# A hybrid flow-matching backbone: the high parts of the mixers' weights come by a second, casting load

## The chip, the cores and the metric

One NeuronCore of a Trainium2 chip runs the whole kernel. The metric is the device time of one execution in microseconds (us). The kernel before takes 2733.23 us (median of 3 runs, 2732.98 to 2734.27).

## What is computed

The reference is a backbone of four layers on 256 latent tokens and 256 context tokens, 1024 features wide. Cut to what matters here:

```python
for i in range(4):
    mod_l, mod_c = silu(c) @ ada_w[i] + ada_b[i], silu(c_ctx) @ ada_w[i] + ada_b[i]   # six vectors each
    h  = modulate(rmsnorm(x, norm_mix[i]), shift, scale)         # context and latents
    o  = (gated_deltanet, rglru, hgrn2)[i % 3](h @ w_in, ...) @ w_out
    x  = x + gate * o
    x  = x + gate2 * (silu(h2 @ w1) * (h2 @ w3)) @ w2            # h2 = modulated rmsnorm of x
return rmsnorm(x_latents, norm_final)
```

Layers 0 and 3 mix the tokens by a gated DeltaNet, layer 1 by the RG-LRU, layer 2 by HGRN2. The last layer needs the latents alone at its end. All inputs and weights are float32.

## The kernel before

Features lie along the 128 partitions, the 512 tokens along the free dimension. Every dense product is carried by three products of split operands: an operand is its high part, rounded to float32r, plus a low part, the exact rest. `dense` (L162 to L173) takes one slab of weights, 128 rows by 8 blocks of 128 columns (512 KB), and for each of 8 blocks multiplies high by high (L170), low weights by high tokens (L171) and high weights by low tokens (L172): 24 matmuls for a slab.

The slabs come in a fixed order, which `plan` writes down. For each slab `load` (L93) sends one DMA on SyncE's queue into one of 4 `raw` tiles. `fetch` (L110) splits it: a copy to the tile `whi` gives the high part, on ScalarE (L123) or, within the RG-LRU's blocks, on VectorE (L121, `hi_dve`); a subtraction on VectorE, raw less `whi`, gives the tile `wlo` (L124). There are 3 tiles `whi` and 3 `wlo`. Splits run 2 slabs ahead of the slab in use and loads 4 slabs ahead, so the `whi` of slab n+2 takes the tile of slab n-1 and has to wait for the last matmul of that one. The projections of the DeltaNet take their slabs with no splitting ahead and call `fetch` after the convolution that follows (L634, L642).

The mixers use 41 slabs of weights in layer 0, 28 in layer 1, 48 in layer 2 and 41 in layer 3 (their input, gate and output weights). The feed-forward parts use 68 slabs a layer (`w13`, `w2`). Beside these, the modulation weights `ada` come through the same 4 `raw` tiles in layer 0's mixer (48 loads in all before and in it, the first 16 into tiles of their own), where TensorE multiplies them by silu(c) (L286); the later layers' ada weights come beside a feed-forward part, into tiles of their own.

The order of the instructions of each engine's queue is set when the program is built, by a scheduler that goes by its own estimate of each instruction's time; within the RG-LRU's blocks ScalarE keeps the order of the program text. On the chip each queue runs in that order, and an instruction that waits holds up what is queued behind it. GpSimd issues no DMA in this kernel. It does elementwise work: products with a sigmoid (L535), masks (L245), products in HGRN2 (L1237, L1238, L1255) and in the RG-LRU (L1046, L1081, L1113, L1122), and half of the norms' products (L385).

Of the kernel before, what the change touches and what calls it, by code (L numbers as in the profile page):

```python
"""Hybrid flow-matching backbone on one NeuronCore.

Everything runs feature-major: a stream of 512 tokens (256 context, then 256 latent) lies along
the free dimension, features along the partitions in blocks of 128. Dense float32 products are
carried by three single-pass float32r products of exactly split operands.
"""
# [14 lines left out]
P = 128  # L21
KT = 8
T = 512
# [31 lines left out]
class Net:  # L55
# [9 lines left out]
    # ---------------------------------------------------------------- weights  # L65
    AHEAD, AHEAD_RAW = 2, 4

    def plan(self):
        """Every slab of weights, in the order in which the layers take them."""
# [33 lines left out]
    def take(self, *key, ahead=None):  # L103
        """The next slab [128 k, kt x 128 n] as high and low parts; later ones are set going."""
        assert self.wplan[self.wpos][0] == key[0] and self.wplan[self.wpos][1] == key[1:], (key, self.wplan[self.wpos])
        self.wpos += 1
        self.fetch(self.AHEAD if ahead is None else ahead)
        return self.wready.pop(0)

    def fetch(self, ahead=AHEAD):  # L110
        """Loads and splits of the slabs up to `ahead` past the last one taken."""
        nc = self.nc
        n = len(self.wplan)
        while self.wsplit_at < min(n, self.wpos + ahead):
            while self.wload_at < min(n, self.wsplit_at + 1):
                self.wload()
            t, w = self.wraw.pop(0)
            hi = self.p_w.tile([P, 1024], F32R, tag="whi", name=self.nm("whi"))
            lo = self.p_w.tile([P, 1024], F32R, tag="wlo", name=self.nm("wlo"))
            if self.hi_dve:  # L120
                nc.vector.tensor_copy(hi[:, :w], t[:, :w])  # L121
# [8 lines left out]
    def wload(self):  # L130
# [8 lines left out]
        self.wraw.append((self.load(src, w), w))  # L139
        self.wload_at += 1  # L140

    # ---------------------------------------------------------------- building blocks
# [17 lines left out]
    def dense(self, w, hs, t0=0, t1=T, ps=None):  # L160
        """ps[n, t] = sum_k w[k, n] h[k, t] over the blocks of hs = [(hi, lo)]."""
# [13 lines left out]
    def dense2(self, k1, k2, hs, ps1, ps2):  # L175
        """Two dense products, both for the context first: its half of hs is there earlier."""
# [6 lines left out]
    def gather(self, po):  # L183
        """A product that adds to a part of the bank po. The first one makes all of the bank ready
        to be written, so the others stay behind it."""
# [16 lines left out]
    def sigmoid(self, out, in_):  # L202
        """1 / (1 + exp(-x)) from the table set that also has the logarithm."""
# [5 lines left out]
    # ---------------------------------------------------------------- constants  # L209
    def consts(self, pool):  # L210
# [11 lines left out]
        # column s adds up over the partitions  # L222
# [12 lines left out]
        # allowed [p, i]: i >= p forwards, i <= p backwards  # L235
# [5 lines left out]
    def causal(self, out, in_, d, n, chunks=1, fill=0.0):  # L241
        """out[p, .., i] = in_ where i >= p (forwards) or i <= p (backwards), else fill."""
# [4 lines left out]
    # ---------------------------------------------------------------- modulation  # L247
    def ada(self, i, summed):
        """Generator: the six modulation vectors of layer i, a piece of the weights at a time.

        Either by products, or (summed) on the vector engine, which leaves the sum over the
        partitions to the products."""
# [3 lines left out]
        for g in range(3):  # L256
# [22 lines left out]
            else:  # L279
                # half of the columns of both vectors at a time: the first blocks of features go on early  # L280
# [11 lines left out]
    def ada_out(self, i, g, ps, js):  # L292
        """The vectors' blocks js from the rows 32 j of the bank ps, feature-major and with their bias."""
# [19 lines left out]
    def step_ada(self, n=1):  # L313
        """Up to n steps."""
# [7 lines left out]
    # ---------------------------------------------------------------- norms  # L322
# [6 lines left out]
    def stats_add(self, n, s):  # L329
        """Squares of the feature block n, stream s, as soon as it is final."""  # L330
# [12 lines left out]
    def rstd(self, s):  # L343
        """1 / sqrt(mean over the features + eps) of stream s, on every partition."""
# [9 lines left out]
    def behind(self, ins, first):  # L354
        """Keep ins behind an earlier instruction of its engine."""
# [1091 lines left out]
```

## Time and profile before

| | |
|---|---|
| median of 3 runs | 2733.23 us |
| span of the profiled execution | 2732.4 us, 0.8 us under that median; the page gives no other time for it |
| TensorE matmul busy | 2576.3 us, 94% of the span |
| VectorE busy | 1846.4 us, 68% |
| ScalarE busy | 1257.2 us, 46% |
| GpSimd busy | 330.1 us, 12% |
| moved by DMA | 373.66 MB, 137 GB/s over the span |

The span falls into eight stretches: a mixer and its output product, then a feed-forward part, for each layer. The mixers lie at 0 to 475 us (layer 0), 835 to 1050 (layer 1), 1411 to 1806 (layer 2) and 2170 to 2530 (layer 3); the feed-forward parts lie between them and at the end. A stretch is read from the table of busy times, which engine is nearly always busy in it, and from the chain of work that ended last, which says what each step was released by. Names carry the layer and stage: L1m is the mixer of layer 1, L3kq the keys and queries of layer 3, L0f the feed-forward part of layer 0, op an output product.

### The profile page before, as it was taken

To read this page: it belongs to the slowest core of one execution; us is meant where nothing else is said; L and a number is where in the kernel's file an instruction comes from. 1 tells how busy PE (TensorE), PEld (TensorE's weight loads), DVE (VectorE), ACT (ScalarE), POOL (GpSimd) and SP (SyncE) were. 2 spreads that over 40 slices of the span, in tenths; PEclk is the share of its full clock that TensorE was granted. 3 is DMA by queue.
4 is the path that set the end of the run, shared out by engine and by line. 5 is a ranking of instruction groups with operands and counts; after the bars stand their busy time and mean duration, and the time that the engine had idled before them with its cause. 6 is when DMAs were issued, how large, how long until landed. Compare 5 with 4: busy or idle time off the path is not lost.

```text
span 2732.4 us, 39594 instructions
## 1 busy us (share of the span) xinstructions
PE 2576.3 (94%) x15528; PEld 2137.5 (78%) x15528; DVE 1846.4 (68%) x2851; ACT 1257.2 (46%) x2075; POOL 330.1 (12%) x286
## 2 busy tenths in 40 slices
PE   7999899999999889999999999999999997788998
PEld 3676788888878668888878888788888786678998
DVE  4585866666667986766666656667666668566555
ACT  4567664322236654222245545442222465774443
POOL 1331001000002421000012122110000134110000
PEclk9999999999999989999999999999999998989999
DMA  6675432555542224555522212135555454224554
GB/s 232 209 228 167 140 122 94 162 169 176 172 140 91 77 70 124 185 169 164 175 85 78 62 62 77 56 124 183 163 177 167 130 152 123 79 70 142 163 181 129
DMA packets 129515, 373.66 MB, mean 137 GB/s; under 512 B 13712, under 2 KB 24976, under 8 KB 129328
## 3 DMA queue, kind: packets, MB, share of 16 engines
q1 hardware_dynamic: 128176, 369.03, 43.3%
q8 instruction: 122, 2.00, 0.3%
q10 hardware_dynamic: 1152, 2.10, 0.2%
q14 instruction: 65, 0.53, 0.1%
HBM read 355.28 MB, written 15.79 MB: 136 GB/s over the span
## 4 chain that ended last, share of the span: by engine, by line
PE 71%; DVE 12%; ACT 8%; DMA 4%; issue 3%; POOL 2%; SPq 0%; ACTq 0%; POOLq 0%; DVEq 0%
PE L0f_psm L172 3%; PE L0f_psm L170 3%; PE L0f_psm L171 3%; PE L2f_psm L170 3%; PE L2f_psm L172 3%; PE L1f_psm L170 3%; PE L1f_psm L172 3%; PE L2f_psm L171 3%; PE L1f_psm L171 3%; PE L3f_psm L172 1%; PE L3f_psm L171 1%; PE L3f_psm L170 1%; PE L2m_psd L172 1%; PE L0f_psd L172 1%; PE L0f_psd L170 1%
## 5 line engine op out<-in xcount | busy, mean ns | idle before, releaser
L123 ACT ACTIVATE L0f_whi<-L0f_raw 128x1024 fp32r<-128x1024 f32 (+1 forms) x58 | 61.2, 1054 | 229.0 <-issue 139.8
L123 ACT ACTIVATE L1f_whi<-L1f_raw 128x1024 fp32r<-128x1024 f32 (+1 forms) x58 | 61.2, 1054 | 228.7 <-issue 143.7
L123 ACT ACTIVATE L2f_whi<-L2f_raw 128x1024 fp32r<-128x1024 f32 (+1 forms) x58 | 61.1, 1054 | 228.7 <-issue 143.7
L269 DVE SCALAR_TENSOR_TENSOR L1f_acc<-L1f_raw,silu_c,L1f_acc 128x1024 f32<-128x1024 f32 x84 | 107.6, 1281 | 42.1 <-DMA L1f_raw<-in_ada 41.9
L269 DVE SCALAR_TENSOR_TENSOR L0f_acc<-L0f_raw,silu_c,L0f_acc 128x1024 f32<-128x1024 f32 x84 | 107.6, 1281 | 40.6 <-DMA L0f_raw<-in_ada 40.5
L269 DVE SCALAR_TENSOR_TENSOR L2f_acc<-L2f_raw,silu_c,L2f_acc 128x1024 f32<-128x1024 f32 x84 | 107.6, 1281 | 39.8 <-DMA L2f_raw<-in_ada 39.7
L124 DVE TENSOR_TENSOR L3f_wlo<-L3f_raw,L3f_whi 128x1024 fp32r<-128x1024 f32 (+1 forms) x58 | 70.5, 1216 | 50.5 <-ACT L3f_whi L123 50.5
L172 PE MATMUL L2m_psd<-hlo,L2m_whi 128*128 128x512 f32 (+1 forms) x256 | 103.7, 405 | 0.0
L123 ACT ACTIVATE L3f_whi<-L3f_raw 128x1024 fp32r<-128x1024 f32 (+1 forms) x58 | 61.0, 1052 | 91.4 <-issue 59.1
L171 PE MATMUL L2m_psd<-hhi,L2m_wlo 128*128 128x512 f32 (+1 forms) x256 | 101.2, 395 | 0.9 <-DVE L2m_wlo L124 0.9
L170 PE MATMUL L2m_psd<-hhi,L2m_whi 128*128 128x512 f32 (+1 forms) x256 | 100.0, 391 | 0.0
L171 PE MATMUL L1f_psm<-hhi,L1f_wlo 128*128 128x512 f32 (+1 forms) x248 | 95.0, 383 | 0.2 <-DVE L1f_wlo L124 0.2
L171 PE MATMUL L2f_psm<-hhi,L2f_wlo 128*128 128x512 f32 (+1 forms) x248 | 95.0, 383 | 0.2 <-DVE L2f_wlo L124 0.2
L171 PE MATMUL L0f_psm<-hhi,L0f_wlo 128*128 128x512 f32 (+1 forms) x248 | 95.0, 383 | 0.2 <-DVE L0f_wlo L124 0.2
L172 PE MATMUL L1f_psm<-hlo,L1f_whi 128*128 128x512 f32 (+1 forms) x248 | 94.9, 383 | 0.0
L170 PE MATMUL L1f_psm<-hhi,L1f_whi 128*128 128x512 f32 (+1 forms) x248 | 94.9, 383 | 0.0
L172 PE MATMUL L2f_psm<-hlo,L2f_whi 128*128 128x512 f32 (+1 forms) x248 | 94.9, 383 | 0.0
L170 PE MATMUL L0f_psm<-hhi,L0f_whi 128*128 128x512 f32 (+1 forms) x248 | 94.9, 383 | 0.0
L170 PE MATMUL L2f_psm<-hhi,L2f_whi 128*128 128x512 f32 (+1 forms) x248 | 94.9, 383 | 0.0
L172 PE MATMUL L0f_psm<-hlo,L0f_whi 128*128 128x512 f32 (+1 forms) x248 | 94.7, 383 | 0.0
L124 DVE TENSOR_TENSOR L2m_wlo<-L2m_raw,L2m_whi 128x1024 fp32r<-128x1024 f32 x38 | 50.0, 1315 | 36.3 <-ACT L2m_whi L123 36.0
L124 DVE TENSOR_TENSOR L0f_wlo<-L0f_raw,L0f_whi 128x1024 fp32r<-128x1024 f32 (+1 forms) x58 | 70.2, 1210 | 1.6 <-ACT L0f_whi L123 1.5
(1330 smaller groups left out, 8724.8 us busy)
## 6 DMA issues: line engine op xcount, KB each, us to landing
L0f_raw<-in_w SPq DMA_DIRECT2D x56, 512.0 KB, 4.4
L1f_raw<-in_w SPq DMA_DIRECT2D x56, 512.0 KB, 4.5
L2f_raw<-in_w SPq DMA_DIRECT2D x56, 512.0 KB, 4.4
L3f_raw<-in_w SPq DMA_DIRECT2D x56, 512.0 KB, 3.6
L0f_raw<-in_ada SPq DMA_DIRECT2D x48, 512.0 KB, 3.8
L1f_raw<-in_ada SPq DMA_DIRECT2D x48, 512.0 KB, 3.9
L2f_raw<-in_ada SPq DMA_DIRECT2D x48, 512.0 KB, 3.8
L2m_raw<-in_w_hin SPq DMA_DIRECT2D x36, 512.0 KB, 3.5
```

The source lines that it names most:

```text
L123: nc.scalar.activation(hi[:, :w], t[:, :w], AF.Copy)
L124: nc.vector.tensor_tensor(out=lo[:, :w], in0=t[:, :w], in1=hi[:, :w].bitcast(F32), op=ALU.subtract)
L170: mm(o, wh, hh[:, t0:t1], start=(k == 0), stop=False)
L171: mm(o, wl, hh[:, t0:t1], start=False, stop=False)
L172: self.pe_mark = mm(o, wh, hl[:, t0:t1], start=False, stop=(k == n - 1))
L269: ins = nc.vector.scalar_tensor_tensor(out=o, in0=w, scalar=c, in1=o, op0=ALU.mult, op1=ALU.add)
```

## The change

A second way to the high part is added for the slabs of the mixers: instead of the copy from `raw`, GpSimd issues a DMA that reads the same slab from HBM again and writes it as float32r, rounded on the way, into `whi`. The load into `raw` stays, and so does the subtraction for `wlo`. The feed-forward slabs keep ScalarE's copy. The flag `hi_dve` goes, and with it VectorE's copies. Comments are left out too, which changes no instruction.

```diff
+    CAST = ("w_gab", "w_gin", "w_gout", "w_lin", "w_lg", "w_lout", "w_hin", "w_hout")
...
-            t, w = self.wraw.pop(0)
+            t, w, src, cast = self.wraw.pop(0)
             hi = self.p_w.tile([P, 1024], F32R, tag="whi", name=self.nm("whi"))
             lo = self.p_w.tile([P, 1024], F32R, tag="wlo", name=self.nm("wlo"))
-            if self.hi_dve:
-                nc.vector.tensor_copy(hi[:, :w], t[:, :w])
+            if cast:
+                nc.gpsimd.dma_start(hi[:, :w], src)
             else:
                 nc.scalar.activation(hi[:, :w], t[:, :w], AF.Copy)
             nc.vector.tensor_tensor(out=lo[:, :w], in0=t[:, :w], in1=hi[:, :w].bitcast(F32), op=ALU.subtract)
...
-        self.wraw.append((self.load(src, w), w))
+        self.wraw.append((self.load(src, w), w, src, name in self.CAST))
...
-                self.hi_dve = True
                 with tc.manual_schedule(engines={mybir.EngineType.Activation}):
                     self.lru_blocks(i, t2, neg, pos, hs)
-                self.hi_dve = False
```

## Rows read from the trace of the kernel before

**Rows 1.** Busy by stretch: window, length, PE, PEld, DVE, ACT, POOL, clock, DMA share, GB/s.

```profile
0.00:475.00 475.00, 432.25 (x3089) 322.15 (x3090) 311.67 (x641) 285.01 (x510) 89.27 (x93) 0.98 0.53 171
475.00:835.00 360.00, 359.88 (x1647) 294.43 (x1647) 239.38 (x274) 102.01 (x136) 0.74 (x1) 1.00 0.52 161
835.00:1050.00 215.00, 187.96 (x871) 154.45 (x870) 188.70 (x261) 136.04 (x225) 71.20 (x47) 0.91 0.25 79
1411.00:1806.00 395.00, 379.51 (x2373) 320.47 (x2372) 259.60 (x424) 206.09 (x351) 80.12 (x67) 1.00 0.22 69
2170.00:2530.00 360.00, 301.47 (x2663) 263.41 (x2662) 250.12 (x548) 233.45 (x453) 81.42 (x76) 0.92 0.37 112
```

**Rows 2.** The same view inside layers 0, 1 and 3.

```profile
0.00:40.00 40.00, 22.60 (x85) 9.62 (x86) 19.41 (x45) 19.14 (x43) 11.10 (x21) 0.87 0.97 356
74.00:215.00 141.00, 134.46 (x657) 94.83 (x655) 104.94 (x164) 79.91 (x126) 49.56 (x45) 0.99 0.71 226
892.83:928.15 35.32, 31.29 (x126) 24.99 (x125) 34.54 (x39) 23.37 (x35) 13.88 (x9) 0.90 0.23 75
928.15:963.47 35.32, 28.32 (x115) 22.18 (x113) 34.54 (x39) 23.41 (x36) 13.84 (x9) 0.90 0.24 75
2170.00:2280.00 110.00, 100.63 (x623) 86.47 (x622) 83.72 (x154) 79.29 (x151) 44.15 (x44) 0.97 0.47 140
```

**Rows 3.** Chain that ended last, 835 to 1010 us: shares by line; then pieces (start, length, what).

```profile
by line: DVE L1m_g L1113 8.1%; DVE L1m_wlo L124 7.4%; DVE L1m_whi L121 6.9%; DVE L1m_xc L508 6.9%; issue 6.5%; DVE L1m_t L1123 5.2%; DVE L1m_t L1116 5.1%; PE L1m_psd L172 4.7%; PE L1m_psd L170 4.2%; PE L1m_psd L171 4.0%; DVE L1m_t L1119 3.9
...
893.34 1.32 DVE L1m_whi L121
...
920.78 0.69 DVE L1m_whi L121
```

**Rows 4.** Waits of PE in layer 1: total us, times, longest.

```profile
PE L1m_psd L171 <- DVE L1m_wlo L124: 6.8, 2, 3.4
```

**Rows 5.** The same chain, one head of layer 3's keys and queries, and the next head's product.

```profile
2222.69 0.95 ACT L3kq_whi L123
...
2225.57 1.31 POOL L3n_kT L535
...
2236.77 1.30 POOL L3n_kT L535
```

**Rows 6.** The same chain, one head of layer 2.

```profile
1515.45 0.95 ACT L2m_whi L123
```

**Rows 7.** Timeline: first and last matmul of one slab in layer 2.

```profile
1532.35 0.40 PE L170 MATMUL L2m_psd<-hhi,L2m_whi 128*128 128x512 f32 x1
...
1537.59 0.39 PE L172 MATMUL L2m_psd<-hlo,L2m_whi 128*128 128x512 f32 x1
```

**Rows 8.** Split and issue of layer 1's slabs: ns min/median/max, first and last start.

```profile
L124 DVE TENSOR_TENSOR L1m_wlo<-L1m_raw,L1m_whi x18: 1193/1222/2285, 865.7 to 982.9; 128x1024 fp32r<-128x1024 f32 x18
L95 SPq DMA_DIRECT2D L1m_raw<-in_w_lin x12: 327/328/328, 845.3 to 931.8; - x12
```

**Rows 9.** DMA issues: destination<-source, queue, count, size, median us to landing.

```profile
L0kq_raw<-in_ada SPq DMA_DIRECT2D x19, 512.0 KB, 4.6
c_raw<-in_ada SPq DMA_DIRECT2D x8, 512.0 KB, 7.3
L1m_raw<-in_w_lin SPq DMA_DIRECT2D x12, 512.0 KB, 3.6
```

**Rows 10.** The chain in layer 0: first and last ada load in it, of six.

```profile
75.45 4.44 DMA L0kq_raw<-in_ada
...
211.91 4.81 DMA L0v_raw<-in_ada
```

**Rows 11.** POOL's products (L535 and L1238): ns min/median/max, or busy us and mean ns.

```profile
L535 POOL TENSOR_TENSOR L3v_vacc<-L3v_vacc,L3v_e x8: 1267/1278/6053, 2305.2 to 2452.0; 128x512 f32<-128x512 f32 x8
...
L1238 POOL TENSOR_TENSOR L2m_qdd<-L2m_gcum,L2m_q 128x512 f32<-128x512 f32 x16 | 27.6, 1741 | 0.0
```

**Rows 12.** Waits of DVE on loads in layer 0's feed-forward part: total us, times, longest.

```profile
DVE L0f_acc L269 <- DMA L0f_raw<-in_ada: 40.5, 34, 2.8
```

More of the change, by code (lines that the diff above doesn't have):

```diff
@@ L1313, in run @@
             self.wplan, self.wpos, self.wsplit_at, self.wload_at = self.plan(), 0, 0, 0
-            self.wraw, self.wready, self.hi_dve, self.nbank, self.p_ada, self.mark = [], [], False, 0, None, None
+            self.wraw, self.wready, self.nbank, self.p_ada, self.mark = [], [], 0, None, None
             self.consts(pc)
```

## Prediction

> **What bounds the kernel now.** I read the busy times by stretch first. In a feed-forward part TensorE is busy for all but 0.1 us of 360 [rows 1]; the change leaves these parts alone, and they are not looked at further. What it can move lies in the mixers, where TensorE has idle time: 42.8 us of 475 in layer 0, 27.0 of 215 in layer 1, 15.5 of 395 in layer 2 and 58.5 of 360 in layer 3 (length less PE busy) [rows 1]. Those 143.8 us are an outer bound on any gain, but for the lower clock, 0.91 and 0.92 in layers 1 and 3 [rows 1], which can rise where TensorE waits less.
>
> Next I read which engine is full inside a mixer. Layer 1 repeats a period of 35.32 us, and VectorE is busy for 34.54 us of it while TensorE is busy for 28.3 to 31.3 [rows 2]: this stretch is VectorE's. Layer 0 is different. Its first 40 us run with the DMA engines at 0.97 and 356 GB/s, and from 74 to 215 us they are at 0.71 [rows 2]. Layer 2 is TensorE's, 379.5 of 395 [rows 1]. Layer 3 is nobody's: it is a chain that goes from engine to engine, so a microsecond on any of them may count. The chain of waits, read third, says which splits stand on that path.
>
> **The change part by part.** The mixers have 41 + 28 + 48 + 41 = 158 slabs. Each loses one copy and gains one DMA on GpSimd's queue. All times below are against the profiled span of 2732.4 us; the median is 0.8 us above it, and I add the same change to the median.
>
> *Layer 1, copies removed from VectorE.* The copies L121 have 6.9% of the 175 us of the chain from 835 to 1010, which is 12.1 us; five of them, 4.9 us, lie in each of the two full periods [rows 3]. Without them VectorE needs 34.5 - 4.9 = 29.6 us for the period. TensorE's own need is the next bound: five slabs (four of projections, one of gates) of 24 matmuls each, at a distance of (1537.59 - 1532.35)/23 = 0.228 us [rows 7], make 120 x 0.228 = 27.4 us. So VectorE stays the bound, the period can go from 35.3 to about 30.4 us, and the full gain is the 12.1 us. TensorE's two waits of 3.4 us for `wlo` [rows 4] are part of it, because there the subtraction stands behind a late copy. Against it stands a new wait: the subtraction now needs the casting load. I take 10 of the 12.1; the bounds are -15 (some copies off the chain count too) and 0.
>
> *Is there time for the load?* The tile `whi` of slab n+2 is released when slab n-1 is through; slab n+2 is used two slabs later, 2 x 24 x 0.228 = 10.9 us where slabs follow one another without a gap [rows 7]. What must fit is GpSimd's issue, the transfer and the subtraction. GpSimd issues no DMA before, so the issue has no row: SyncE's takes 0.33 us [rows 8], one of GpSimd's own products takes 1.74 [rows 11]. I take 1.0, between them. The nearest load of the same bytes lands 3.6 us after its issue in layer 1 [rows 9], 7.3 in the full stretch at the start. The subtraction takes 1.22 us [rows 8]. That is 1.0 + 3.6 + 1.2 = 5.8 us of 10.9, with 5 us left for GpSimd and VectorE being busy. So TensorE does not wait for these loads as a rule. The Trainium skill (DMA: Bandwidth & Descriptors, Latency and other measured facts) gives about 1 us to the first byte for a DMA that GpSimd issues and 0.6 for one that SyncE issues; by that figure as an estimate the load would land 0.4 us later than SyncE's, and the sum would be the same. No row here shows it.
>
> *Layer 3, copies removed from ScalarE.* In the keys and queries of each head the chain runs through ScalarE's copy: 0.95 us of `whi` ahead of the sigmoid, and then GpSimd's product [rows 5]. It stands there once for a head of 11.2 us, eight heads, 7.6 us. TensorE idles 9.4 us of that stretch [rows 2], so this can be won. The rest of layer 3, its values and output product, has 25 slabs more, with copies that are mostly off the chain; I give them 2 us. What is added is GpSimd's issue, and GpSimd's product of 1.3 us stands on the same chain [rows 5]: two issues for a head, some in front of it. I take 2.5 us back. Net -7, bounds -12 and +9 (two issues of 1.0 us for each of eight heads all in the chain, less the 7 us).
>
> *Layer 2, copies removed from ScalarE.* One copy of 0.95 us stands on the chain for each head, 7.6 us for eight [rows 6]. But TensorE idles only 15.5 us of 395 [rows 1], and the work beside it is next; I take half, -4. Bounds -8 and +4 (GpSimd's queue: its two products of 1.74 us for each head come behind an issue that waits for TensorE's release of `whi`; they feed TensorE a good deal later).
>
> *Layer 0, loads added.* Here nothing is won on VectorE, and ScalarE's copies are seldom on the chain; I take -1. What is added is 41 slabs of 0.5 MB. At the start all three `whi` tiles are free, so 0.26 + 0.52 + 0.52 = 1.31 MB go out on GpSimd's queue in the first microseconds, into the stretch that runs at 356 GB/s with the DMA engines full [rows 2]: 1.31/0.356 = 3.7 us later for what is queued behind, and the products of the ada weights wait for that. From 74 to 215 us some 18 casting loads (14 of keys and queries, 4 of values and gates) come into a share of 0.71. At 356/0.97 = 367 GB/s a load takes 1.43 us of all engines, 18 x 1.43 = 25.7 us of 141, and the share goes to 0.89. Not full, but an ada load lands later: 4.6 us now, 7.3 in the full stretch [rows 9]. Six of them are steps of the chain there [rows 10]. I take +0.55 us each, +3.3; the upper bound is 6 x 2.7 = +16. A raw tile is also held until the subtraction, some 4 us longer, which SyncE's queue feels since ada loads wait for the same four tiles; that is inside the bound. Sum for layer 0: +3.7 + 3.3 - 1 = +6, bounds -1 and +20.
>
> *At no cost:* the `raw` loads of the mixers remain as they are; in layers 1 to 3 the DMA engines are at 0.25, 0.22 and 0.37 [rows 1], and 28, 48 and 41 loads more of 1.43 us make 40 us of 215, 69 of 395 and 59 of 360, that is shares of 0.44, 0.40 and 0.53. If that cover were gone, layer 0's prices would hold there too.
>
> The sum: -10 - 7 - 4 + 6 = -15 us. From 2733.2 that is **2718 us**, 0.5% faster.
>
> **The rivals.** *Same: GpSimd becomes part of the path.* The 158 issues go through a queue that does everything else in order. In layer 3 and layer 0 its product L535 is on the chain, and if an issue takes the 1.74 us of its own longest usual work [rows 11] and stands in front of that product, two for each of sixteen heads and half of them in the way, it is 16 x 1.74 = 28 us, less what gaps hide. At about 15 us the gain is gone: 2733 us. For it speaks that the issue is unknown; against it that GpSimd is busy for 81 us of 360 in layer 3 [rows 1].
>
> *Slower: VectorE stands waiting at the subtraction.* The place is VectorE's queue in layer 1 and in the keys and queries of layer 3. The subtraction stands where the scheduler thinks the load has landed. If it lands later, VectorE, which is the bound, idles with all its other work behind. Such a wait is there before, on loads: 34 times in one feed-forward part, 40.5 us, 1.2 us each [rows 12]. With 28 + 16 = 44 slabs at 1.2 us it is 53 us, 38 net of the 15 won: 2771 us. It decides from 15/44 = 0.34 us for each slab. Against it speaks that VectorE's order is made with the load's time in mind, and that there is a margin of 5 us before TensorE needs the slab; a smaller wait, 0.8 us each, gives 2753.
>
> *Late descriptors.* One product of GpSimd took 6.05 us where the others took 1.28 [rows 11], so VectorE can hold GpSimd up. If every issue in layer 1 took 6.05 us, 6.05 + 3.6 + 1.2 = 10.9 us would use up all of the margin, and layer 1's 10 us would be lost: 2728 us. The Trainium skill (SBUF — State Buffer, SBUF: two separate sides and Who interferes with whom) has a rule against this change: while VectorE runs a copy in its two-port mode GpSimd can't write the descriptors of its DMA; a two-input operation blocks only those GpSimd instructions that read SBUF. By that rule the copies which do the blocking in layer 1 are largely the ones that go. No row here shows a DMA of GpSimd's.
>
> *Layer 0's loads* at their upper bound of +20 give 2732 us, no change.
>
> **How the numbers follow.** Forecast 0.56; GpSimd on the path 0.13; VectorE waiting 0.24; late descriptors 0.03; layer 0 at its bound 0.04. A measurement of this kernel can tell 0.2%, 5.5 us, from no change. Faster is the forecast, 0.56; same is the first, third and fourth rival, 0.20; slower is the second, 0.24. The forecast's own range is 2700 to 2727: the lower bounds together are -15 - 12 - 8 - 1 = -36 us, 2697, and hardly all come at once. The range that holds 8 in 10 runs from 2700 to 2748, which takes in the cases without change and nearly half of the slower one.
>
> **What would show it.** Layer 1's period from 35.3 to about 31 us, with VectorE still above 0.95 and no L121; if it stays and the waits of VectorE name a DMA into `whi`, the second rival holds. In layer 3 no ScalarE copy in the chain of the keys and queries, and a head in about 10.3 us for 11.2. In layer 0 a mean landing of the ada loads above 4.6 us and an end of the mixer some 6 us later. GpSimd's issue near 1 us; far more would make the first rival true. Layer 2 within 8 us of now. The forecast is wrong if the waits of VectorE on these loads come to over 15 us in all, or if layer 0 loses more than 20.

## The result, and the profile after

The changed kernel takes 2845.69 us (median of 4 runs, 2843.21 to 2861.55) against 2733.69 us before in the same series; the ratio is 1.042, with a 95% interval from 1.0405 to 1.0435. It is 112 us slower, where 15 us less was forecast. The span of its profiled execution is 2841.8 us, against 2732.4. In its code the casting load is L123, ScalarE's copy (feed-forward slabs alone) L125, the subtraction L126 and the three products of a slab L172 to L174.

From the page, the busy times of the engines, and the new queue (packets, MB, share of 16 engines):

```profile
PE 2620.1 (92%) x15528; PEld 2165.7 (76%) x15528; DVE 1843.2 (65%) x2830; ACT 1141.6 (40%) x1938; POOL 410.5 (14%) x444
q0 software_dynamic: 22752, 82.32, 9.6%
```

What was meant to go is gone: ScalarE is busy for 1141.6 us, 115.6 less than before. Yet TensorE, with the same number of products, is busy for 2620.1 us, 43.8 more, and 65.6 of the 109.4 us are time in which it does nothing. The busy times by stretch, which answer to [rows 1] (mixer and output product of layers 0 to 3; columns as there, but cut at the first product of each stage), say where:

```profile
0.00:505.10 505.10, 434.68 (x3023) 318.73 (x3024) 303.42 (x624) 241.55 (x453) 106.42 (x131) 0.95 0.62 200
879.50:1083.30 203.80, 173.78 (x780) 138.93 (x779) 160.89 (x220) 121.88 (x198) 71.75 (x69) 0.93 0.46 143
1458.20:1890.20 432.00, 395.86 (x2299) 332.64 (x2299) 259.29 (x410) 158.79 (x288) 102.93 (x109) 0.93 0.37 116
2264.90:2635.70 370.80, 303.32 (x2639) 265.19 (x2637) 247.70 (x542) 196.43 (x407) 100.29 (x112) 0.91 0.54 165
```

For the rest of the text the span is cut at the first product of each stage, since both kernels issue the same products. The first column of numbers is the length before, the others are differences to it. The runs beside the changed kernel are described below; each column is one profiled execution, named as its run without the number.

```
stage                     before  changed  touch  dram  dram2    low   whx  whxo   opx   l1x    l1  l1x4
layer 0, mixer+output      464.3    +40.8   +0.6 +25.0  +26.3  +27.6 +40.1 +40.6 +42.9  +3.0  +4.3  +3.1
layer 0, feed-forward      373.7     +0.7   -0.1  +0.0   +0.2   +0.6  +0.7  +0.4  +0.5  +0.7  +1.0  +0.8
layer 1, mixer             140.5     -2.0   -0.2  +0.6   -0.4   +2.8  -8.5  -8.4  -2.7  -8.7  -2.9  -8.4
layer 1, output product     60.9     +4.4   -1.1  +0.1   +0.7   -0.5  -2.2  -2.2  +9.1  -2.2  +3.1  -1.0
layer 1, feed-forward      374.1     +0.8   +0.0  +0.0   +0.0   +0.7  +0.9  +0.8  +0.6  -0.2  -0.2  -0.7
layer 2, mixer             342.6    +46.3  +19.4 +13.2   +0.7  +38.5 +18.7  +8.5 +55.6  +1.4  +1.7  +1.2
layer 2, output product     41.8     +1.3   -0.0  -0.1   +0.0   +1.5  +0.9  +2.2  -0.8  +0.0  -0.1  +0.0
layer 2, feed-forward      373.7     +1.0   +0.2  +0.2   +0.0   +0.9  +1.0  +0.8  +0.4  +0.0  +0.1  +0.2
layer 3, keys and queries  109.5     +3.9   -1.5  +1.6   +3.3   +7.4  +1.2  +1.1  +0.3  +0.0  +0.0  -1.5
layer 3, values, chains    219.4     +6.1   -0.2  -1.9   +1.9   +3.4  +8.8  +5.0  +9.3  +0.2  +0.4  +0.9
layer 3, output product     27.3     +4.6   +1.0  -0.9   -0.1   +4.7  +5.1  +4.7  -1.0  +0.0  -1.3  -0.1
layer 3, feed-forward      204.6     +1.5   +0.1  +0.6   +0.8   +0.4  +0.3  +0.2  +0.3  +0.9  +1.5  +0.5
sum                       2732.4   +109.4  +18.2 +38.4  +33.4  +88.0 +67.0 +53.7 +114.5  -4.9  +7.6  -5.0
```

Two layers lose four fifths of it: layer 2 with +46.3 us in its mixer, and layer 0 with +40.8. Layer 3 loses 14.6, layer 1 2.4, and the four feed-forward parts 4.0 together. A single figure of this table is good to some 4 us: layer 0 is 3.0 to 4.3 us longer in the last three columns, where it holds no casting load at all and VectorE, ScalarE and GpSimd have its instructions in the order of before. What these 3 to 4 us are was not found. Where the clock falls, a figure is less sharp still: in layer 2's mixer `changed` and `opx` have the same waits of TensorE for `qe` (15.9 us), and yet differ by 9.3 us, 8.1 of them TensorE being busy longer at a mean clock of 0.90 instead of 0.92.

**The loads.** The rows of the casting issue give its duration on GpSimd (ns, min/median/max), and the list of DMA issues the time from the start of an issue to the landing (us, last column; the ada rows answer to [rows 9]):

```profile
L123 POOL DMA_DIRECT2D L2m_whi<-in_w_hin x39: 530/570/593, 1456.8 to 1803.5; - x39
...
L2m_whi<-in_w_hin POOLq DMA_DIRECT2D x39, 512.0 KB, 4.0
L2m_raw<-in_w_hin SPq DMA_DIRECT2D x36, 512.0 KB, 3.7
L1m_whi<-in_w_lin POOLq DMA_DIRECT2D x15, 512.0 KB, 4.5
L0kq_raw<-in_ada SPq DMA_DIRECT2D x19, 512.0 KB, 5.8
```

An issue costs GpSimd 0.57 us, and in layers 2 and 1 the load lands 4.0 and 4.5 us after its start, 0.3 and 0.7 us more than SyncE's of the same bytes there (3.7 and 3.8). So for these two layers none of the sizes assumed for the load was wrong. In the keys and queries of layers 3 and 0 it lands after 5.4 and 6.0 us (SyncE's: 4.5 and 6.2). The 4.0 us stand where ScalarE's copy took 0.95 [rows 6]: the high part is there some 3 us later after TensorE's release of the tile.

**The waits** of layer 2's mixer (engine, line, waited for: us in total, times, longest):

```profile
PE L2m_psm L1242 <- DVE L2m_qe L1235: 15.9, 4, 4.0
PE L2m_psd L191 <- DVE L2m_q L1208: 7.1, 4, 2.3
...
PE L2m_psd L173 <- DVE L2m_wlo L126: 0.4, 1, 0.4
...
POOL L2m_whi L123 <- PE L2m_psd L174: 144.9, 25, 14.1
...
DVE L2m_wlo L126 <- DMA L2m_whi<-in_w_hin: 25.1, 19, 3.6
```

TensorE hardly waits for a slab, 0.4 us. It waits for the mixer's own values `qe` and `q`, which VectorE makes, and VectorE waits for the loads. GpSimd stands for 144.9 us at the head of its queue for TensorE's release. Which of these two long waits carries the loss is what the experiments ask. The timeline of VectorE shows how the load gets at `qe`. Before the change, ahead of TensorE's products of one head:

```profile
1569.05 1.22 DVE L124 TENSOR_TENSOR L2m_wlo<-L2m_raw,L2m_whi 128x1024 fp32r<-128x1024 f32 x1
...
1571.38 0.68 DVE L1236 TENSOR_TENSOR L2m_ke<-L2m_ke,L2m_sig 128x512 f32<-128x512 f32 x1
1571.98 3.45 DVE L1235 TENSOR_TENSOR L2m_qe<-L2m_qe,L2m_q 128x512 f32<-128x512 f32 x2
1575.36 0.91 DVE L1246 COPY_PREDICATED AT<-hm,L2m_psm 64x256 f32<-64x256 uint32 x2
1576.30 1.38 DVE L124 TENSOR_TENSOR L2m_wlo<-L2m_raw,L2m_whi 128x1024 fp32r<-128x1024 f32 x1
```

The same place after it:

```profile
1633.04 0.68 DVE L1236 TENSOR_TENSOR L2m_ke<-L2m_ke,L2m_sig 128x512 f32<-128x512 f32 x1
1633.64 2.29 DVE L126 TENSOR_TENSOR L2m_wlo<-L2m_raw,L2m_whi 128x1024 fp32r<-128x1024 f32 x1
1635.86 3.42 DVE L1235 TENSOR_TENSOR L2m_qe<-L2m_qe,L2m_q 128x512 f32<-128x512 f32 x2
```

The subtraction at 1633.64 is the counterpart of the one at 1569.05: in both kernels its slab's high part can start when the projection of the queries has left its tile. Before, it stood three products earlier in VectorE's queue, ahead of `ktt`, `q` and `ke`, in part in time in which VectorE would have waited for ScalarE's `q` and `ke` (their last steps ended at 1570.32 and 1570.83). Now it stands directly ahead of `qe`, though nobody needs its slab yet. It takes 2.29 us there, with products of GpSimd beside it, and TensorE's wait for `qe` goes from 1.4 to 4.0 us for each pair of heads. An earlier subtraction of the head stands ahead of the scan L1224 in the same way. The next load goes out later still, because GpSimd's own products stand ahead of its issue. TensorE's last product with the slab that frees its tile ended at 1633.18, the issue starts 5.5 us after that, and VectorE stands for 1.72 us until the load has landed:

```profile
1637.02 1.71 POOL L1238 TENSOR_TENSOR L2m_qdd<-L2m_gcum,L2m_q 128x512 f32<-128x512 f32 x1
1638.68 0.59 POOL L123 DMA_DIRECT2D L2m_whi<-in_w_hin  x1
```

```profile
1642.53 1.23 DVE L126 TENSOR_TENSOR L2m_wlo<-L2m_raw,L2m_whi 128x1024 fp32r<-128x1024 f32 x1 [1.72 <-DMA L2m_whi<-in_w_hin]
```

Behind each of the four waits of 4.0 us for `qe` the clock falls. Around the first of them, TensorE's busy time, granted clock, DMA share and GB/s in four stretches of 4 us:

```profile
1540.00:1544.00 4.00, 1.39 (x5) 1.00 0.12 50
1544.00:1548.00 4.00, 2.29 (x22) 0.76 0.46 135
1548.00:1552.00 4.00, 4.00 (x37) 0.81 0.45 131
1552.00:1556.00 4.00, 4.00 (x26) 1.00 0.39 131
```

Of the mixer's 46.3 us, 25.2 are TensorE being busy longer (354.30 us for 329.15 at the same products, mean clock 0.92 for 1.00), and 21.1 are idle time.

### The profile page after: what moved, and what is told of

Its sections match the earlier page's. It is cut to its first block, busy times and chain, and to the rows that moved or that the text cites. A ratio compares the mean times of both kernels' runs of the same rounds, so it can differ in the third digit from the quotient of the medians.

```text
span 2841.8 us, 39836 instructions
## 1 busy us (share of the span) xinstructions
PE 2620.1 (92%) x15528; PEld 2165.7 (76%) x15528; DVE 1843.2 (65%) x2830; ACT 1141.6 (40%) x1938; POOL 410.5 (14%) x444
## 5 line engine op out<-in xcount | busy, mean ns | idle before, releaser
L125 ACT ACTIVATE L0f_whi<-L0f_raw 128x1024 fp32r<-128x1024 f32 (+1 forms) x58 | 61.2, 1055 | 229.0 <-issue 139.8
L125 ACT ACTIVATE L2f_whi<-L2f_raw 128x1024 fp32r<-128x1024 f32 (+1 forms) x58 | 61.2, 1055 | 228.6 <-issue 143.7
L125 ACT ACTIVATE L1f_whi<-L1f_raw 128x1024 fp32r<-128x1024 f32 (+1 forms) x58 | 61.2, 1055 | 228.6 <-issue 143.7
L172 PE MATMUL L2m_psd<-hhi,L2m_whi 128*128 128x512 f32 (+1 forms) x256 | 102.7, 401 | 2.2 <-ACT L2m_vtok L1193 1.9
L126 DVE TENSOR_TENSOR L3f_wlo<-L3f_raw,L3f_whi 128x1024 fp32r<-128x1024 f32 (+1 forms) x58 | 70.5, 1216 | 50.2 <-ACT L3f_whi L125 50.2
L174 PE MATMUL L2m_psd<-hlo,L2m_whi 128*128 128x512 f32 (+1 forms) x256 | 103.1, 403 | 0.0
L125 ACT ACTIVATE L3f_whi<-L3f_raw 128x1024 fp32r<-128x1024 f32 (+1 forms) x58 | 61.0, 1052 | 91.4 <-issue 59.1
L174 PE MATMUL L1f_psm<-hlo,L1f_whi 128*128 128x512 f32 (+1 forms) x248 | 94.8, 382 | 0.0
L174 PE MATMUL L2f_psm<-hlo,L2f_whi 128*128 128x512 f32 (+1 forms) x248 | 94.8, 382 | 0.0
L172 PE MATMUL L1f_psm<-hhi,L1f_whi 128*128 128x512 f32 (+1 forms) x248 | 94.7, 382 | 0.0
L172 PE MATMUL L2f_psm<-hhi,L2f_whi 128*128 128x512 f32 (+1 forms) x248 | 94.7, 382 | 0.0
L172 PE MATMUL L0f_psm<-hhi,L0f_whi 128*128 128x512 f32 (+1 forms) x248 | 94.7, 382 | 0.0
L174 PE MATMUL L0f_psm<-hlo,L0f_whi 128*128 128x512 f32 (+1 forms) x248 | 94.6, 382 | 0.0
L126 DVE TENSOR_TENSOR L2m_wlo<-L2m_raw,L2m_whi 128x1024 fp32r<-128x1024 f32 x38 | 57.1, 1503 | 47.7 <-DMA L2m_whi<-in_w_hin 25.1
L126 DVE TENSOR_TENSOR L0f_wlo<-L0f_raw,L0f_whi 128x1024 fp32r<-128x1024 f32 (+1 forms) x58 | 70.2, 1210 | 1.6 <-ACT L0f_whi L125 1.5
```

The costliest lines, as they stand in the source:

```text
L125: nc.scalar.activation(hi[:, :w], t[:, :w], AF.Copy)
L126: nc.vector.tensor_tensor(out=lo[:, :w], in0=t[:, :w], in1=hi[:, :w].bitcast(F32), op=ALU.subtract)
L172: mm(o, wh, hh[:, t0:t1], start=(k == 0), stop=False)
L174: self.pe_mark = mm(o, wh, hl[:, t0:t1], start=False, stop=(k == n - 1))
```

## The experiments

Theory A: the high part comes later after the release of its tile, so the subtractions move in VectorE's queue to places ahead of the mixer's own work, and wait there. Rival B: GpSimd's own products are held up behind an issue that waits for TensorE. Rival C: the traffic of the second loads.

**Waiting without loading (e1_touch).** The kernel before, with one write ahead of the copy:

```diff
+            if cast:
+                nc.gpsimd.memset(hi[:, 0:1].bitcast(F32), 0.0)
             if self.hi_dve:
```

> The kernel before (high parts copied on ScalarE and VectorE), but ahead of each copy of a mixer's slab GpSimd writes one column of the tile whi; this write waits at the head of GpSimd's queue until TensorE has released the tile, as the casting issue does, but nothing is loaded. Theory A (the high part comes too late: issue 0.57 us plus landing 4.0 us after the release in layer 2, for a copy of 0.95 us, and the subtraction and what stands behind it on VectorE shift): about 2735 us, no layer moves by more than 5 us. Rival B (GpSimd's own products stand behind the waiting instruction): most of the loss of 112 us is there, 2790 to 2845 us, with layer 2 some 30 to 48 us longer. Rival C (the second load's traffic): 2735 us.

Measured: 2756.35 us (2751.79 to 2764.47), ratio 1.0085 (1.0063 to 1.0108). Layer 2's mixer is 19.4 us longer and nothing else moves, which neither theory expected: A said no more than 5, B at least 30. What TensorE waits for in it is ScalarE's copy `ktok`, and ScalarE's own queue tells why; first a row of the waits, then the timelines of GpSimd and ScalarE:

```profile
PE L2m_psm L1270 <- ACT L2m_ktok L1254: 8.2, 4, 2.1
```

```profile
1489.78 3.42 POOL L1241 TENSOR_TENSOR L2m_qdd<-L2m_gcum,L2m_q 128x512 f32<-128x512 f32 x2
1493.14 0.09 POOL L122 MEMSET L2m_whi<- 128x1 f32 x1
```

```profile
1493.26 1.06 ACT L126 ACTIVATE L2m_whi<-L2m_raw 128x1024 fp32r<-128x1024 f32 x1 [3.85 <-POOL L2m_whi L122]
```

(The expectation counts the issue twice: the 4.0 us run from its start.) GpSimd's products are not late. The write stands behind them for 3.4 us, and ScalarE, whose copy waits for the write, stands for 3.85 us with `ktok` behind it. In the change ScalarE copies no slab of the mixers, so it has no such wait; the experiment had a flaw of its own, and B needed another one (e8). It does show how little it takes: 5.6 us of idle time more in the whole mixer, and 13.8 us of lower clock.

**The traffic beside it (e2_dram).** The same, and a casting DMA of the same bytes that nobody reads:

```diff
+                spare = self.p_dram.tile([P, 1024], F32R, tag="spare", bufs=8, name=self.nm("spare"))
+                self.behind(nc.gpsimd.dma_start(spare[:, :w], src), first)
```

> As the run before it (a write of one column of whi on GpSimd ahead of the copy), and behind each such write GpSimd issues a casting DMA of the same bytes into a spare tensor in DRAM that nobody reads: traffic and issue at the time of the changed kernel, without anyone who waits for the load. Theory A (lateness): the traffic matters in layer 0 alone, +5 to +15 us there, layer 2 within 5 us: 2740 to 2750 us. Rival B (GpSimd's queue): as the touch alone plus 1 us or so a head. Rival C (traffic): layer 0's mixer +30 to +41 us, layer 3 +10 or more, 2780 us or more in all.

Measured: 2789.24 us (2772.62 to 2801.34), ratio 1.0192 (1.0152 to 1.0232); the profiled execution, with a span of 2770.8, is the shortest of them. Layer 0 is 25.0 us longer, more than A's 15, less than C's 30 and than the 40.8 of the change; layers 1 and 3 are where they were, and layer 2 has +13.2 by the flaw of the run before, since ScalarE's copy waits for the same write. The spare tensor lies in DRAM and is written in longer pieces than the tile would be, so the traffic is the same in bytes alone.

**Neither held up nor waited for (e8_dram2).** The kernel before with those DMAs, no write to `whi`, and the issue waiting for TensorE's last product before the slab's turn:

```diff
+                spare = self.p_dram.tile([P, 1024], F32R, tag="spare", bufs=8, name=self.nm("spare"))
+                ins = nc.gpsimd.dma_start(spare[:, :w], src)
+                if self.pe_last is not None:
+                    self.tc.add_manual_dep(ins.ins, self.pe_last.ins.name, mybir.DependencyInfo(mybir.DependencyClass.Sync, mybir.DependencyReason.DATA), reason="release")
```

> The kernel before, with the casting DMAs into a spare tensor in DRAM and no write to whi: GpSimd's issue waits for TensorE's last product before the slab's turn, which is the point of release, and nobody waits for issue or load. In the earlier run of this kind ScalarE's copy waited behind GpSimd's write to whi, up to 3.85 us while GpSimd was at its two products, which is a cost that the change doesn't have in this form. Theory A (GpSimd's own products are hardly delayed by the waiting issue, the loads cost only through contention): layer 2 within 4 us of before, layer 0 +20 to +27, 2755 to 2765 us. Rival B (products behind the waiting issue): layer 2 +13 us or more, 2770 us or more.

Measured: 2766.51 us (2759.86 to 2768.1), ratio 1.0113 (1.0098 to 1.0127), 1.5 us above A's range and 3.5 below B's. Layer 2's mixer, its busy times and two rows of its waits:

```profile
1440.30:1783.60 343.30, 329.56 (x2081) 276.17 (x2079) 226.54 (x360) 180.00 (x299) 89.97 (x100) 1.00 0.41 129
```

```profile
PE L2m_psm L1248 <- DVE L2m_qe L1241: 5.7, 4, 1.4
...
POOL L2m_spare L123 <- PE L2m_psd L178: 127.4, 20, 8.6
```

GpSimd waits at the head of its queue for 127.4 us, nearly as long as in the change, the DMA share is 0.41, and the mixer is 0.7 us longer: rival B falls, and rival C falls for layer 2 as far as reads from HBM and bytes go. These loads write DRAM, where those of the change write SBUF; what that could cost is bounded by the 8.5 us that layer 2 still loses in e7 below, whose loads write SBUF too. Layer 0 is 26.3 us longer, which is the price of the loads alone there. Layer 3 has 5.2 us of it before its output product.

**Another order (e3_low).** The changed kernel, with a lower priority for the subtraction when the queues are made:

```diff
+            at = self.tc.cur_priority
+            self.tc.cur_priority = at + (200 if cast else 0)
             nc.vector.tensor_tensor(out=lo[:, :w], in0=t[:, :w], in1=hi[:, :w].bitcast(F32), op=ALU.subtract)
+            self.tc.cur_priority = at + 1
```

> The changed kernel, but the subtraction of a cast slab has a lower priority by 200 instructions when the queues' order is made. In layer 2 the third subtraction of a head then stands behind the product qe L1235, for which TensorE waits 3.97 us for each pair of heads (1.42 before), instead of ahead of it, and the first one behind the scan L1224. Theory A with the order on VectorE as the way in which lateness costs: TensorE's wait for qe goes back to 1.4 us in each pair, 4 x 2.5 = 10 us, and the clock gives some of it again: 2846 - 10 to 2846 - 25 us, so 2821 to 2836. Rivals B and C: nothing changes, 2846 us within 4.

Measured: 2818.06 us (2812.12 to 2822.72), ratio 1.03 (1.0281 to 1.032): 28 us less than the change, more than expected. TensorE's wait for `qe` in layer 2 goes from 15.9 to 8.8 us, 2.2 for each pair of heads where 1.4 was expected. The mixer gives 7.8 us, no more than two executions with the same waits did differ by; it is the wait that shows what the order does. Layer 0 gives 13.2, and stands with +27.6 at the price of the loads alone (e8: +26.3). So layer 0's loss is the loads, about 26 us, and VectorE's order, about 14, by one execution of each.

**Loads that go out earlier (e4_whx).** More tiles, so that the load doesn't wait for the slab just finished:

```diff
+            pool = self.p_w
+            if cast and self.p_hi:
+                self.nhi = (self.nhi + 1) % (3 + self.p_hi[1])
+                pool = self.p_w if self.nhi < 3 else self.p_hi[0]
-            hi = self.p_w.tile([P, 1024], F32R, tag="whi", name=self.nm("whi"))
+            hi = pool.tile([P, 1024], F32R, tag="whi", name=self.nm("whi"))
...
-                    self.hgrn(i, perm)
+                    with tc.tile_pool(name="whx2", bufs=1) as p_hi:
+                        self.p_hi = p_hi, 1
+                        self.hgrn(i, perm)
+                    self.p_hi = None
...
-                            both = p.tile([P, 4, P], F32, tag="both", name=self.nm("both"))
+                            both = p.tile([P, 4, P], F32, tag="both", bufs=1, name=self.nm("both"))
```

> The changed kernel with more tiles whi: four in layer 2 (one buffer of the tile both is given up for it), five in layer 1; layers 0 and 3 have no room and stay. The casting load of a slab then needs no release by the slab just finished, and goes out one slab (5.5 us) or two earlier. Theory A (lateness): layer 2 comes back to within 10 us of before (-38 us or more against the changed kernel), layer 1 to 5 to 12 us less than before: 2790 to 2805 us in all. Rival B (GpSimd's queue blocked): the same, since the issue no longer blocks; the touch tells A from B. Rival C (traffic): unchanged, 2846 us, since the same bytes move.

Measured: 2801.57 us (2798.05 to 2812.52), ratio 1.0248 (1.0226 to 1.027). Layer 1 turns into the gain that was forecast, 10.7 us less than before (-8.5 and -2.2). Layer 2's mixer gets 27.6 of its 46.3 us back, at the same traffic, but not the 36 and more that A had promised. Of these, 14.5 are idle time and 13.1 TensorE's busy time (341.25 us). The rest shows mostly in TensorE's clock, in stretches of 4 us behind one pair of heads:

```profile
1524.00:1528.00 4.00, 2.93 (x23) 1.00 0.20 27
1528.00:1532.00 4.00, 2.95 (x24) 0.67 0.62 236
1532.00:1536.00 4.00, 4.00 (x15) 0.50 0.00 0
1536.00:1540.00 4.00, 4.00 (x15) 0.50 0.00 0
1540.00:1544.00 4.00, 4.00 (x16) 0.50 0.00 0
1544.00:1548.00 4.00, 4.00 (x19) 0.69 0.00 0
1548.00:1552.00 4.00, 4.00 (x19) 1.00 0.02 4
```

In the first two stretches TensorE waits, 1.0 us for `qe` and 2.1 us for the state `S`, and then it runs at 0.50 (1.2 GHz) for some 15 us. That is the longest of the four: behind the same two waits in the other three pairs the clock is below 1.00 in one or two such stretches. VectorE's timeline of this run shows a subtraction again in front, now of the predicated copies (it is the next one in the queue, since the one that stood ahead of `qe` in the change now starts at 1517.86), and GpSimd's shows what runs beside it:

```profile
1524.87 2.30 DVE L130 TENSOR_TENSOR L2m_wlo<-L2m_raw,L2m_whi 128x1024 fp32r<-128x1024 f32 x1
1527.10 0.88 DVE L1250 COPY_PREDICATED AT<-hm,L2m_psm 64x256 f32<-64x256 uint32 x2
```

```profile
1524.37 1.73 POOL L1242 TENSOR_TENSOR L2m_qdd<-L2m_gcum,L2m_q 128x512 f32<-128x512 f32 x1
```

**Earlier loads and a subtraction held back (e7_whxo).** The same kernel, with one subtraction of each head held back on VectorE:

```diff
-            nc.vector.tensor_tensor(out=lo[:, :w], in0=t[:, :w], in1=hi[:, :w].bitcast(F32), op=ALU.subtract)
+            self.last_lo = nc.vector.tensor_tensor(out=lo[:, :w], in0=t[:, :w], in1=hi[:, :w].bitcast(F32), op=ALU.subtract)
...
-                            nc.vector.copy_predicated(at[q_, :, q_], mask[d][q_].unsqueeze(1).to_broadcast([64, 4, CH]), scv[q_])
+                            ins = nc.vector.copy_predicated(at[q_, :, q_], mask[d][q_].unsqueeze(1).to_broadcast([64, 4, CH]), scv[q_])
+                        if d == 0:
+                            self.behind(self.last_lo, ins)
```

> The run with more tiles (four in layer 2, five in layer 1), and in layer 2 the subtraction of the last slab that a head fetches is held behind the predicated copies of that head's first direction on VectorE, where it stands before the change; without that it stands ahead of them, takes 2.30 us beside a product of GpSimd, and TensorE's wait for the state S is 2.1 us in each pair of heads, the wait for qe 1.0, with the clock falling behind them. Theory A (VectorE's order is the rest of layer 2's loss): layer 2's mixer from +18.7 us against before to +8 or less, TensorE's wait for S under 1 us in each pair, 2801.6 - 11 = 2791 us or less. Rival (the order isn't it: GpSimd's queue or the traffic): layer 2 stays at +15 to +19, 2798 to 2803 us.

(The edit does more than it says. The subtraction that it holds, the last that a head fetches, stood ahead of `qe` before the change, at 1569.05 above; held behind the copies, it pushes the next one, which was in the way at 1524.87, behind them too.)

Measured: 2792.96 us (2787.82 to 2797.51), ratio 1.0213 (1.0197 to 1.023). Layer 2's mixer stands at +8.5 us at a mean clock of 0.98, just outside A's bound and far from the rival's. The profiled execution is the shortest of the four, 5.1 us under the median. TensorE's wait for `S` is 1.1 us in each pair, for 2.1 before this edit:

```profile
1524.97 0.90 DVE L1250 COPY_PREDICATED AT<-hm,L2m_psm 64x256 f32<-64x256 uint32 x2
1525.90 1.37 DVE L130 TENSOR_TENSOR L2m_wlo<-L2m_raw,L2m_whi 128x1024 fp32r<-128x1024 f32 x1
```

```profile
PE L2m_psm L1246 <- DVE L2m_qe L1239: 4.6, 4, 1.2
PE L2m_pso L195 <- DVE L2m_S L1283: 4.2, 4, 1.1
PE L2m_psd L195 <- DVE L2m_q L1212: 4.2, 4, 1.2
```

The places of two subtractions give 10.2 us, with loads that are released by the same slabs. The medians give 8.6, and all four times lie below all four of e4. Of the 10.2, 1.8 us are idle time and 8.4 are TensorE's busy time (332.82 us for 341.25), as much as two executions with the same waits did differ by: that the order is worth something is shown, its size is not sharp. So of layer 2's 46.3 us, 27.6 go with the earlier load and about 10 with the order. Of the last 8.5, 4.8 are idle time, mostly longer waits for `S` and `q`; what makes them, or whether the buffer of `both` that was given up has a part in them, was not taken apart.

**Layer 1 alone (e6_l1, e5_l1x, e10_l1x4).** Casting loads in layer 1 alone, ScalarE's copies elsewhere, with three, five and four tiles there:

```diff
-    CAST = ("w_gab", "w_gin", "w_gout", "w_lin", "w_lg", "w_lout", "w_hin", "w_hout")
+    CAST = ("w_lin", "w_lg", "w_lout")
```

> Casting loads in layer 1 alone, three tiles whi as in the change. Theory A: layer 1 as in the changed kernel, -2.0 us in the mixer and +4.4 in the output product, 2734.7 + 2.4 = 2737 us (2733 to 2741); the difference to the run with five tiles, some 13 us, is the lateness of the load. Rival (layers act on one another): as far off as 2724 us or below.

> Casting loads in layer 1 alone, with five tiles whi there; layers 0, 2 and 3 copy on ScalarE as before. Theory A (the removed copies are worth what was forecast where the load comes early enough, and layers don't act on one another): the run with more tiles had layer 1's mixer 8.5 us and its output product 2.2 us shorter than before, so 2734.7 - 10.7 = 2724 us, bounds 2718 to 2729, faster than the kernel before. Rival (the gain there hangs on the other layers, or is noise): 2734 us within 3.

> Casting loads in layer 1 alone with four tiles whi there, between the three of the change (+0.2 us in layer 1's mixer and output product together) and five (-10.9 us). Theory A (the load needs the lead of a whole slab, and a second one brings little): -7 to -11 us in layer 1, 2727 to 2731 us. Rival (only two slabs of lead cover the load): within 3 us of 2739 as with three tiles.

Measured: three tiles 2739.46 us, ratio 1.0015 (1.0006 to 1.0025); five tiles 2729.1, ratio 0.9978 (0.9968 to 0.9988); four tiles 2731.27, ratio 0.9986 (0.9977 to 0.9996). In the table, layer 1's mixer and output product together are at +0.2, -10.9 and -9.4 us. So what layer 1 gains doesn't hang on the other layers, and one tile more is nearly all that is needed; with the casting load in place, the same removed copies are worth nothing or 10 us by when the load can start. The totals of the runs with five and four tiles lie at the upper end of what was expected, 0.1 and 0.3 us above it. Left untested is the plain rival: more tiles for the kernel before, with VectorE's copies as they are. How much of the gain the tiles alone would give is not known. That the medians gain only 5.4 and 2.9 us is for about half layer 0's 3 us, spoken of above; the rest is spread over the other stages. The version with five tiles is the shortest kernel of this study, 0.2% under the one before. Layer 1's mixer in it, and below it that of the kernel before:

```profile
841.70:973.50 131.80, 119.31 (x534) 96.12 (x533) 113.25 (x146) 96.58 (x153) 57.34 (x55) 0.96 0.49 156
```

```profile
838.00:978.50 140.50, 123.21 (x534) 99.97 (x533) 131.78 (x164) 96.39 (x153) 53.83 (x35) 0.91 0.23 72
```

**Output products (e9_opx).** The changed kernel with five tiles in the output products alone (the pool of two more opened in `out_proj`):

```diff
-        with self.tc.tile_pool(name=self.nm("norm"), bufs=1) as pool:
+        with self.tc.tile_pool(name=self.nm("whx"), bufs=2) as p_hi, self.tc.tile_pool(name=self.nm("norm"), bufs=1) as pool:
+            self.p_hi, self.nhi = (p_hi, 2), 2
```

> The changed kernel with five tiles whi in the output products alone, where the mixers' working tiles have been given back and there is room in every layer. Theory A (lateness): TensorE's wait of 3.3 us for the casting load in layer 3's output product goes, and the output products come back from +4.4 (layer 1), +1.3 (layer 2) and +4.6 (layer 3) against before to -2 to +1 each; the rest of the layers as in the changed kernel: 2846 - 10 = 2836 us (2831 to 2841). Rival (what is late there isn't the load but the end of the mixer before it): within 3 us of 2846.

Measured: 2839.28 us (2837.67 to 2848.65), ratio 1.0386 (1.0368 to 1.0403), 6.4 us under the change and inside A's bounds. The profiled execution is the longest of the four, and its layer 2 mixer, whose waits for `qe` are those of the change (15.9 us), is 9 us longer at a clock of 0.90. In the output products of layers 2 and 3 the loss is gone, +1.3 to -0.8 and +4.6 to -1.0; in the changed kernel TensorE had this wait in layer 3, which the run no longer has:

```profile
PE L3op_psm L172 <- DMA L3op_whi<-in_w_gout: 3.3, 1, 3.3
```

In layer 1 the output product is longer still, +9.1: there TensorE waits 7.9 us for the last value of the mixer, for 9.5 us in the change and 4.6 before it. That part of the expectation fell; there the rival holds, what is late in layer 1 is the mixer's end. Why the output product is longer than in the change is not shown.

## Why the prediction was wrong, by its steps

**Layer 1, -10 us; measured +2.4.** The term was worth what it was said to be worth, 10.9 us, in the run where loads start earlier (e5). That the size fits so well is luck in part: the mixer's 8.7 us are 4.8 of idle time and 3.9 of TensorE's busy time (119.31 us for 123.21, at a clock of 0.96 for 0.91), and 2.2 come from the output product; the sum had VectorE's time alone. VectorE did lose its copies in the change (busy 131.78 us before and 113.81 after in the mixer), but the mixer went from 140.5 to 138.5 us only: VectorE waits 9.0 us for loads instead, and TensorE for slabs (5.7 us for `wlo` and 2.4 us for the load, at the gates).

**Is there time for the load? This is the step that failed.** Its sizes were right for layers 1 and 2: issue to landing 4.0 to 4.5 us and a subtraction of 1.2 make 5.2 to 5.7, for 5.8 forecast. Its 10.9 us are the time until TensorE needs the slab, and in layer 2 TensorE waited for a slab for 0.4 us. But the first consumer is not TensorE. It is the subtraction in VectorE's queue, which runs in order, with the mixer's chain behind it. Only that place counts, and it has no such margin: VectorE's waits for casting loads sum to 122 us over the kernel (18 rows of the waits, 60 times). This sum is a sign and not a price: in layer 2, where 46.3 us are lost, the waits are 25 us, and the subtraction that delays `qe` waits for nothing.

**Layer 2, -4 us, bounds -8 and +4; measured +47.6 with its output product.** The step saw ScalarE's copy go, which was right, and bounded the cost by GpSimd's products behind the issue. That bound holds: 0.7 us (e8). What it left out is that the copy also held the subtraction at its place in VectorE's order. A subtraction that comes 3 us later lands directly in front of `qe`, and takes 2.3 us there instead of 1.2. And that TensorE idles for only 15.5 us of 395 [rows 1] was read as little to win; it should have been read as much to lose, since the mixer ran at a clock of 1.00 with no wait of TensorE over 1.6 us. Over half of the loss, 25.2 us, is the clock, which has no term in the sum.

**Layer 0, +6 us, bounds -1 and +20; measured +40.8.** The start behaved as said: its first products with layer 0's weights come 3.4 us later (35.5 for 32.1), for 3.7. The ada loads land 1.2 us later each (5.8 for 4.6 [rows 9]), for 0.55 taken, and TensorE's waits for them in the keys and queries go from 3.4 us to 15.0. The stretch of values and chains, at a DMA share of 0.46, was given no cost at all; in e8 the time from the first values to the output product grows by 10.9 us. With these the loads come to 26.3 us in e8, over the upper bound, and VectorE's order is some 14 us on top of it (e3).

**Layer 3, -7 us, bounds -12 and +9; measured +14.6.** ScalarE's busy time in the keys and queries falls from 79.1 to 63.5 us, but the chain is not shorter (+3.9). The part on what comes at no cost had the DMA shares of layers 1 to 3 right (0.46, 0.37 and 0.54 measured), but the loads are not free in layer 3: the share of its keys and queries goes from 0.48 to 0.72, and e8 has 5.2 us of the loss. Another 5.6 are the late loads of the output product (e9). Both are hardly above the 4 us that a single figure is good to. The rest, about 4 us, was not taken apart.

**The rivals.** GpSimd on the path is refuted at its price of 28 us: an issue takes 0.57 us, not 1.74, and e8, with all the issues, gives 0.7 us in layer 2 and 5.2 in layer 3, the traffic included. What it had the other way round is that the issue comes late behind GpSimd's products, as seen in layer 2. Late descriptors fall too: no issue in layer 1 took over 0.60 us, and the longest of all 158 took 0.72. The rule of the Trainium skill for that rival (SBUF — State Buffer, SBUF: two separate sides), that GpSimd can't write descriptors while VectorE runs a copy in its two-port mode, shows in the duration of no issue. From the first bytes that the Trainium skill gives (DMA: Bandwidth & Descriptors, Latency and other measured facts) the prediction's estimate was 0.4 us more than for SyncE; the landings show 0.3 us more in layer 2, 0.7 in layer 1 and 0.9 in the keys and queries of layer 3, but 0.2 less in those of layer 0. The slower rival named the mechanism, VectorE standing at the subtraction, but as two waits in layers 1 and 3, and it was priced as idle time of VectorE, 53 us, with no part for the clock. What spoke against it, that VectorE's order is made with the load's time in mind, was no protection: the order as it was made has the subtraction directly in front of `qe`. What time the scheduler assumed for the load is not on record.

**What would make it wrong** was named rightly: VectorE's waits over 15 us, and layer 0 over 20. Both came true.

## What to carry to other kernels

When an operation is replaced by a longer but parallel one, measure the margin to the first instruction that waits for it in an in-order queue, not to the engine that uses the result in the end; then ask what stands behind that instruction. In layer 1 such a load needed a buffer more than the copy it replaced: one tile more made the difference between nothing and some 10 us. A stage in which TensorE runs at full clock with small gaps can lose more by a gap of 2 us than its length: in e1, 5.6 us of waits more came with 13.8 us of lower clock.

## What the runs showed of the hardware

GpSimd's issue of a 512 KB casting DMA takes 0.53 to 0.60 us, one of 158 took 0.72. Its load lands 4.0 us after the start of the issue in layer 2's mixer, at a DMA share of 0.37, and 6.0 us after it in layer 0's keys and queries, at 0.78. A subtraction that takes 1.22 us alone took 2.30 beside a product of GpSimd, and that product 1.73, where the shortest of its kind before the change took 1.28. In the changed kernel VectorE's product `qe` took 0.68 to 0.69 us the two times that no product of GpSimd ran beside it, and 1.74 to 1.78 the fourteen times that one did.

TensorE fell to 0.50 of its clock, 1.2 GHz, behind two waits of 1.0 and 2.1 us some 6 us apart in e4, and stayed there for about 15 us in one pair of heads and for less in the other three. In e1 each pair of heads has waits of 1.4 and 2.1 us at 5 us distance: behind those of the first pair the clock stayed at 1.00, behind those of the third it was at 0.50 for some 12 us. One stretch of 4 us behind each:

```profile
1496.00:1500.00 4.00, 3.86 (x42) 1.00 0.43 131
1676.00:1680.00 4.00, 4.00 (x16) 0.50 0.00 0
```

When it falls can therefore not be told from these runs.
